# Value columns of two heads as one Strassen product, the second head's values parked in DRAM

## The chip, the cores and the metric

One Trainium2 chip, one core of it. The metric is the device time of one execution in microseconds (us). Engines by their names in the profile: PE is TensorE's matmuls and PEld its weight loads, DVE is VectorE, ACT is ScalarE, POOL is GpSimd, SP issues the transfers. Lines (L1269) are those of the kernel's file.

## What is computed

One layer of a hybrid decoder: a norm, one input projection for everything, three kinds of head groups side by side, a gate, an output projection with a residual, a last norm. Sizes: 1024 tokens, model width 1024, input projection 1024 x 6160, all in float32.

```python
h = rms_norm(x, norm_w)
proj = h @ w_in                              # (1024, 6160)
gq, gk, gv, glr, hq, hf, hi, xq, gate = split(proj)
gla_o  = rms_norm(chunked_gla(gq, gk, gv, log_decay(glr)))       # 4 heads, keys 128, values 256
hgrn_o = rms_norm(chunked_gla(hq, 1 - f(hf), hi, log f(hf)))     # 4 heads of 128
xo     = rms_norm(softmax(xq @ mk.T) @ mv)                       # 4 heads of 128, 256 memory rows
mixed  = concat(gla_o, hgrn_o, xo) * silu(gate)                  # (1024, 2048)
return rms_norm(x + mixed @ w_out, final_norm_w)
```

The change concerns `gv` (1024 columns, 256 for each of four GLA heads) and `hi` (512 columns, 256 for each pair of HGRN heads): the columns of `proj` that hold values.

## The kernel before

The work goes in eight groups, each of 256 columns of the mixed row: X0, X1 (memory attention, two heads each), G0 to G3 (one GLA head each), H0, H1 (two HGRN heads each). A group first projects what it needs (values, gates, queries, keys), with the list `first[i]` of small units run by `emit`; then its `loop` goes over eight chunks of 128 tokens, and between the chunks it does the output projection of the group before (`out_units`, 96 matmuls in 16 units, each into one of three "pp" banks; the sums go through DRAM: fetched into "acc", added at L1997, written back).

Products are exact to float32 by parts: each operand is kept as a high and a low part, and `mm3` (L1498) issues three matmuls, hi x hi, hi x lo, lo x hi (L1500 to L1502). The normed input is kept in such parts as eight sums of its quarters, `self.A`: A11, A12, A22 and S1 to S4, where the first index is the half of the tokens and the second the half of the 1024 channels. These allow Strassen's form of a 2 x 2 product with seven products (`pair`, L1504, used for gate, queries and keys, where the two column blocks of weights are 128 wide). The token quarters are the matmul's moving side there, 512 wide, and the results lie transposed.

The values come from `v_units` (L1597), one group of 256 columns at a time. There the tokens are the stationary side and the weights move, 256 wide. Half of the tokens is A11, A12; for the other half it uses S1 and A22 with the weights changed (c - a, d - b). A group has six operands a, b, c, d, c - a, d - b: the first two serve all eight token blocks (48 matmuls), the other four serve four (24 matmuls). The results fill the four banks "o", "kv", "sc", "tr" and are copied by ACT (L1627) into the tile "v" (one buffer).

Weights pass through one planner, `Fast.load`, `add`, `prepare`, `w` and `w_done` (L1233 to L1288). A load brings 128 x 512 floats (256 KB) on SP's queue into one of five raw buffers "wst" (`NRAW`). An operand is made from one raw, or from a sum of raws that is done in place (L1262, DVE), and then a cast (L1269, ACT) and a low part (L1270, DVE) into one of five slots "whi"/"wlo" (`NSLOT`). `w(i)` asks for operand i and has two more made ahead (`LOOKAHEAD`). Raw buffers go round, and so do slots: load n takes the buffer of load n - 5 when its last reader is done, operand n the slot of operand n - 5 when its last matmul is done. The order of instructions on each engine is a list made when the kernel is built: units in the order of the source have precedence, but what is not ready yet is overtaken.

Other names in the steps: the tail is what is left of the group before (`step_C`: norm, and two gate units with transposes into the bank "oT", L982, L987); it is run in the first units of the next group's `emit`. The background `bg` holds the pieces that turn gates into decays (`decays`, L1740: scans, two `inverse` of Ln and Exp, L1735 to L1738, and in H groups `keys`, L1862): six pieces in a G group, sixteen in an H group. `emit` (L2064) runs one piece after a unit, in H groups from the 14th unit on after every second one. `gates_gla` (L1697) are the two gate matmuls (L1714) into "pp", read by ACT at L1718 and L1719. "sg" holds four tiles of 128 x 512 (silu of the gates), "h" two, "acc" three.

Of the kernel before, what the change touches and what calls it, by code (L numbers as in the profile page):

```python
# [18 lines left out]
P = 128  # L19
# [1199 lines left out]
class Fast(Trunk):  # L1219
# [35 lines left out]
    def prepare(self, i):  # L1255
# [4 lines left out]
        if sub:  # L1260
            d, a, b = (self.raws[j] for j in sub)
            nc.vector.tensor_tensor(d, a, b, op=ALU.subtract)  # L1262
# [334 lines left out]
    def v_units(self, g, col):  # L1597


        nc, add = self.nc, self.add  # L1600
        a, b = (self.load(("v", col, 256, 0, 4), j) for j in range(2))
        c, d = (self.load(("v", col, 256, 4, 4), j) for j in range(2))
        base = add(a)
        add(b)
        add(c)
        add(d)
        add(c, None, (c, c, a), (a, c))
        add(d, None, (d, d, b), (b, d))
# [455 lines left out]
    def emit(self, g, units):  # L2064
# [3 lines left out]
        for n, u in enumerate(units):  # L2068
# [4 lines left out]
            elif self.bg and (not H or n >= 14 and n % 2 == 0):  # L2073
                self.bg.pop(0)()
# [168 lines left out]
```

## Time and profile before

| | us |
|---|---|
| median of three runs (lowest, highest) | 894.61 (893.73, 897.25) |
| the profiled execution, its own time | 894.56 |
| its span, first to last instruction | 892.8 |
| PE busy | 856.5 (96%) |
| DVE busy | 626.2 (70%) |
| ACT busy | 529.6 (59%) |
| POOL busy | 92.5 (10%) |

Busy times of PE overlap, since matmuls are pipelined and the end of one is modelled; how far apart their starts lie says more. The page cuts the span into 40 slices of 22.3 us. Groups start at about 208 (G0), 306.7 (G1), 406.7 (G2), 505.7 (G3), 605 (H0) and 730 us (H1), each with its values first (in H0 and H1 after the forget gates), then gate and queries, then the loop.

### The profile page before, as it was taken

The numbers are of one execution on the slowest core, as the hardware profiler recorded it, in microseconds if no ns is written. First come the engines' busy times: TensorE is split into PE (matmuls) and PEld (weight loads), VectorE is DVE, ScalarE is ACT, GpSimd is POOL, SyncE is SP. The second block draws the span as 40 slices with busy tenths as digits, with TensorE's granted clock in tenths as the row PEclk, the third lists the DMA queues.
The fourth block names the chain that finished last, engine by engine and source line by source line (L and its number), as shares of the span: only waits on it lengthen the run. The fifth ranks groups of instructions, "written<-read, shape, count | busy, mean of one in ns | idle before, by whom it ended". The sixth has DMA issues, their size and how long they took to land.

```text
span 892.8 us, 13855 instructions
## 1 busy us (share of the span) xinstructions
PE 856.5 (96%) x4742; PEld 714.4 (80%) x4742; DVE 626.2 (70%) x1504; ACT 529.6 (59%) x1273; POOL 92.5 (10%) x111
## 2 busy tenths in 40 slices
PE   8788999999999999999999999999999999999994
PEld 7466887788888898888888898878977878877873
DVE  5879663657648885788648875787685777666676
ACT  4536967987435764467436754466963358942374
POOL 0212112321000110011000110011000011000012
PEclk9989999999999999999999999999999999999997
DMA  9410222451225612472235511473113561034764
GB/s 321 163 48 0 62 69 63 162 199 41 78 84 189 213 49 66 134 236 87 79 107 189 190 60 59 153 229 103 48 48 122 176 208 38 25 110 135 265 220 183
DMA packets 61120, 111.84 MB, mean 125 GB/s; under 512 B 6960, under 2 KB 7088, under 8 KB 61040
## 3 DMA queue, kind: packets, MB, share of 16 engines
q1 hardware_dynamic: 60752, 110.59, 37.4%
q8 instruction: 39, 0.64, 0.3%
q14 instruction: 41, 0.34, 0.1%
q10 hardware_dynamic: 288, 0.28, 0.1%
HBM read 77.28 MB, written 33.55 MB: 124 GB/s over the span
## 4 chain that ended last, share of the span: by engine, by line
PE 69%; DVE 13%; DMA 7%; ACT 7%; issue 3%; SPq 0%; POOL 0%; DVEq 0%; POOLq 0%; ACTq 0%
PE pp L1502 16%; PE pp L1500 16%; PE pp L1501 16%; DMA acc<-sum 3%; DVE acc L1997 2%; PE sc L1500 1%; PE o L1500 1%; DVE A L177 1%; PE sc L1502 1%; DMA A<-w_dram 1%; PE sc L1501 1%; DMA A<-xT_dram 1%; PE oT L982 1%; PE o L1501 1%; PE o L1502 1%
## 5 line engine op out<-in xcount | busy, mean ns | idle before, releaser
L1269 ACT CAST whi<-wst 128x512 fp32r<-128x512 f32 x193 | 117.5, 619 | 181.2 <-PE pp L1501 125.5
L1500 PE MATMUL pp<-A,whi 128*128 128x512 f32 x508 | 203.5, 402 | 3.1 <-ACT A L176 1.5
L1501 PE MATMUL pp<-A,whi 128*128 128x512 f32 x508 | 202.0, 398 | 2.2 <-DVE A L177 2.2
L1502 PE MATMUL pp<-A,wlo 128*128 128x512 f32 x508 | 201.9, 398 | 1.5 <-DVE wlo L1270 1.4
L1270 DVE TENSOR_TENSOR wlo<-wst,whi 128x512 fp32r<-128x512 f32 x193 | 131.7, 689 | 80.9 <-ACT whi L1269 76.3
L1500 PEld LDWEIGHTS pp<-A,whi 128*128 128x128 f32 x508 | 95.8, 189 | 27.5 <-ACT A L176 2.7
L1502 PEld LDWEIGHTS pp<-A,wlo 128*128 128x128 f32 x508 | 95.7, 188 | 26.4 <-DVE wlo L1270 3.6
L1501 PEld LDWEIGHTS pp<-A,whi 128*128 128x128 f32 x508 | 96.0, 189 | 25.6 <-DVE A L177 3.5
L1500 PE MATMUL pp<-whi,mh 128*128 128x512 f32 (+1 forms) x258 | 104.7, 406 | 0.3 <-DVE acc L1997 0.3
L1501 PE MATMUL pp<-wlo,mh 128*128 128x512 f32 (+1 forms) x258 | 102.7, 398 | 0.0
L1502 PE MATMUL pp<-whi,ml 128*128 128x512 f32 (+1 forms) x258 | 101.9, 395 | 0.6 <-POOL ml L992 0.6
L1997 DVE TENSOR_TENSOR acc<-acc,pp 128x512 f32<-128x512 f32 x112 | 76.6, 685 | 31.9 <-PE pp L1502 14.5
L992 POOL TENSOR_TENSOR ml<-h,mh 128x512 fp32r<-128x512 f32 x30 | 41.1, 1369 | 334.4 <-ACT mh L990 334.3
L1262 DVE TENSOR_TENSOR wst<-wst 128x512 f32<-128x512 f32 x82 | 56.9, 694 | 1.5
L1502 PEld LDWEIGHTS pp<-whi,ml 128*128 128x128 f32 x258 | 48.7, 189 | 10.4 <-POOL ml L992 1.0
L1501 PEld LDWEIGHTS pp<-wlo,mh 128*128 128x128 f32 x258 | 48.8, 189 | 7.8 <-DVE wlo L1270 0.3
L1500 PEld LDWEIGHTS pp<-whi,mh 128*128 128x128 f32 x258 | 48.7, 189 | 7.9 <-DVE acc L1997 0.5
L177 POOL TENSOR_TENSOR qk<-qk 128x128 fp32r<-128x128 f32 x28 | 13.0, 470 | 292.8 <-ACT qk L176 253.6
L1955 ACT ACTIVATE o<-o,rs_r 128x128 f32<-128x128 f32 (+1 forms) x96 | 34.2, 427 | 8.7 <-DVE rs_r L195 6.9
L1949 ACT ACTIVATE junk<-o 128x128 bf16<-128x128 f32 (+1 forms) x96 | 32.7, 342 | 1.1
L1946 ACT COPY o<-o 128x256 f32<-128x256 f32 x64 | 23.6, 369 | 15.7 <-PE o L1918 4.7
L990 ACT CAST mh<-h 128x512 fp32r<-128x512 f32 x32 | 19.8, 618 | 21.2 <-DVE h L987 21.1
(278 smaller groups left out, 1860.9 us busy)
## 6 DMA issues: line engine op xcount, KB each, us to landing
wst<-w_dram SPq DMA_DIRECT2D x128, 256.0 KB, 2.6
sum<-acc SPq DMA_DIRECT2D x112, 256.0 KB, 2.1
acc<-sum SPq DMA_DIRECT2D x96, 256.0 KB, 2.8
A<-w_dram SPq DMA_DIRECT2D x16, 256.0 KB, 5.4
A<-xT_dram SPq DMA_DIRECT2D x16, 256.0 KB, 5.4
acc<-x_dram SPq DMA_DIRECT2D x16, 256.0 KB, 2.9
A<-sum SPq DMA_DIRECT2D x16, 256.0 KB, 4.0
out_dram<-A SPq DMA_DIRECT2D x15, 256.0 KB, 2.1
```

Source lines behind the costliest of these rows:

```text
L177: eng.tensor_tensor(to[1], x, to[0].bitcast(F32), op=ALU.subtract)
L992: eng.tensor_tensor(lo, x, hi.bitcast(F32), op=ALU.subtract)
L1262: nc.vector.tensor_tensor(d, a, b, op=ALU.subtract)
L1269: nc.scalar.copy(hi, x)
L1270: nc.vector.tensor_tensor(lo, x, hi.bitcast(F32), op=ALU.subtract)
L1500: mm(out, lhs[0], rhs[0], start=first, stop=False, skip_group_check=skip)
L1501: mm(out, lhs[0], rhs[1], start=False, stop=False, skip_group_check=skip)
L1502: mm(out, lhs[1], rhs[0], start=False, stop=last, skip_group_check=skip)
L1946: nc.scalar.copy(osb, o)
L1949: nc.scalar.activation(junk[:, s * w : (s + 1) * w], osb[:, s], AF.Square, accum_out=g["ss"][:, c % 4, s : s + 1])
L1955: self.nc.scalar.activation(x, x, AF.Copy, scale=r)
L1997: nc.vector.tensor_tensor(dst, dst, ps, op=ALU.add)
```

## The change

The values of two groups (G0 with G1, G2 with G3, H0 with H1) are projected together, by `v_pair` in the first group of each pair, with Strassen's seven products; the two 256-column blocks of weights are the two columns of the 2 x 2 form. Each product has two operands (the two 128-channel pairs of a half), and each operand serves four token blocks, 24 matmuls. The 14 operands of a pair are made from 1, 1, 2, 2, 3, 3, 1, 1, 2, 2, 1, 1, 4, 4 raw loads, 28 in all, and 14 sums (the planner now takes a list of sums, also additions). Six banks are used, the four from before and "oT" and one "pp". Partial results lie in four "sg" tiles (u, u4), and the last ones are added from PSUM by DVE (`plus`) or copied by ACT. The first group's values go to "v" directly, the second group's through an "h" tile to DRAM in four writes of 256 KB. The second group has one unit in the place of its values, `v_load`: four reads of 256 KB into "v". In `emit`, the background of H1 (n = 1) runs after every unit from the 14th on instead of every second one.

```diff
--- before.py
+++ after.py
@@ -1257,9 +1257,9 @@
         raw, need, sub, free, make = self.ops[i]
         while self.n_load <= need:
             self.issue(self.n_load)
-        if sub:
-            d, a, b = (self.raws[j] for j in sub)
-            nc.vector.tensor_tensor(d, a, b, op=ALU.subtract)
+        for *sab, op in [(*sub, ALU.subtract)] if type(sub) is tuple else sub or ():
+            d, a, b = (self.raws[j] for j in sab)
+            nc.vector.tensor_tensor(d, a, b, op=op)
         if make:
             self.slots[i] = make(self.raws[raw])
         else:
@@ -1594,42 +1594,114 @@
 
         return [part(n, q) for n in range(8) for q in range(2)]
 
-    def v_units(self, g, col):
-
-
...
         st = {}
 
-        def part(p, j):
+        def put(e, h, ps, u):
+            for i in range(2):
+                src = ps[i].rearrange("p a b -> p (a b)")
+                if e == 0:
+                    dst = g1["v"][:, 4 * h + 2 * i : 4 * h + 2 * i + 2].rearrange("p a b -> p (a b)")
+                else:
+                    dst = self.t("h", [P, HALF], bufs=2)
+                if u is None:
+                    nc.scalar.copy(dst, src)
+                else:
+                    self.plus(dst, src, u[i])
+                if e:
+                    n = f"v{2 * h + i}"
+                    t = g2.setdefault("vd", {})[2 * h + i] = self.dp.tile([P, HALF], F32, tag=n, name=n)
+                    nc.sync.dma_start(t, dst)
+
+        def done(p):
+            ps = st["ps"]
+            flat = lambda t: t.rearrange("p a b -> p (a b)")
+            if p == 0:
+                st["u"] = [self.t("sg", [P, HALF], bufs=self.sg_bufs) for _ in range(2)]
+                for i in range(2):
+                    nc.scalar.copy(st["u"][i], flat(ps[0][i]))
+            elif p == 2:
+                st["u4"] = [self.t("sg", [P, HALF], bufs=self.sg_bufs) for _ in range(2)]
+                for i in range(2):
+                    self.plus(st["u"][i], flat(ps[2][i]), st["u"][i])
+                    self.plus(st["u4"][i], flat(ps[1][i]), st["u"][i])
+            elif p == 3:
+                put(0, 0, ps[0], None)
+            elif p == 4:
+                put(1, 1, ps[2], st["u4"])
+            elif p == 5:
+                put(1, 0, ps[1], st["u"])
+            elif p == 6:
+                put(0, 1, ps[2], st["u"])
+
+        def part(p, j, i):
             def f():
-                if p == 0 and j == 0:
-                    g["v"] = self.t("v", [P, NB, 256], bufs=1)
-                    st["ps"] = [self.ps(t, [P, 2, 256]) for t in ("o", "kv", "sc", "tr")]
-                whi, wlo = self.w(base + p, 2)
-                name = ("A11" if j < 2 else "S1") if p < 2 else "A12" if p < 4 else "A22"
-                for i in range(2):
-                    sl = slice((2 * j + i) % 4 * P, ((2 * j + i) % 4 + 1) * P)
+                if p == j == i == 0:
+                    g1["v"] = self.t("v", [P, NB, 256], bufs=1)
+                    st["ps"] = [[self.ps(t, [P, 2, 256]) for t in ts] for ts in (("o", "kv"), ("sc", "tr"), ("oT", "pp"))]
+                whi, wlo = self.w(ops[p][j], 2)
+                name, bank = prods[p]
+                for b in range(2):
+                    sl = slice((2 * i + b) * P, (2 * i + b + 1) * P)
                     for k in range(2):
-                        hi, lo = self.A[name][2 * (p % 2) + k]
-                        first, last = p == 0 and i == k == 0, (p == 3 or p == 5) and i == k == 1
-                        self.mm3(st["ps"][j][:, i], (hi[:, sl], lo[:, sl]), (whi[:, k], wlo[:, k]), first, last, True)
-                if j == (1 if p in (2, 3) else 3):
-                    self.w_done(base + p)
-                if p == (3 if j < 2 else 5):
-                    nc.scalar.copy(g["v"][:, 2 * j : 2 * j + 2], st["ps"][j])
+                        hi, lo = self.A[name][2 * j + k]
+                        first = p not in cont and j == b == k == 0
+                        last = j == b == k == 1
+                        self.mm3(
+                            st["ps"][bank][i][:, b], (hi[:, sl], lo[:, sl]), (whi[:, k], wlo[:, k]), first, last, True
+                        )
+                if i == 1:
+                    self.w_done(ops[p][j])
+                    if j == 1:
+                        done(p)
 
             return f
 
-        js = lambda p: range(4) if p < 2 else range(2) if p < 4 else range(2, 4)
-        return [part(p, j) for p in range(6) for j in js(p)]
+        return [part(p, j, i) for p in range(7) for j in range(2) for i in range(2)]
+
+    def v_load(self, g):
+        def f():
+            g["v"] = self.t("v", [P, NB, 256], bufs=1)
+            v = g["v"].rearrange("p a b -> p (a b)")
+            for i in range(4):
+                self.nc.sync.dma_start(v[:, i * HALF : (i + 1) * HALF], g["vd"][i])
+
+        return [f]
+
+    def v_of(self, g, other, base):
+        n = g["n"]
+        if n % 2:
+            return self.v_load(g)
+        return self.v_pair(g, other, base + 256 * n, base + 256 * (n + 1))
 
     def glr_units(self):
 
@@ -2070,7 +2142,7 @@
             if self.tail:
                 if n in (0, 3, 5) or n > 5:
                     self.tail.pop(0)()
-            elif self.bg and (not H or n >= 14 and n % 2 == 0):
+            elif self.bg and (not H or n >= 14 and (g["n"] or n % 2 == 0)):
                 self.bg.pop(0)()
 
     def loop(self, g, fill):
@@ -2116,10 +2188,10 @@
                     n, kind = g["n"], g["kind"]
                     if kind == "G":
                         u = self.glr_units() if n == 0 else []
-                        u += self.gates_gla(g, n) + self.v_units(g, GV + 256 * n)
+                        u += self.gates_gla(g, n) + self.v_of(g, groups[(i + 1) % 8], GV)
                         u += self.gate_units(g) + self.qk_units(g, n)
                     else:
-                        u = self.hf_units(g, n) + self.v_units(g, HI + 256 * n)
+                        u = self.hf_units(g, n) + self.v_of(g, groups[(i + 1) % 8], HI)
                         u += self.gate_units(g) + self.hq_units(g, n)
                     first.append(u)
                 fill.append(self.out_units(groups[i - 1], False))
```

## Rows read from the trace of the kernel before

**Rows 1.** The page: busy time by engine (share, count); granted clock and GB/s by slice

```profile
PE 856.5 (96%) x4742; PEld 714.4 (80%) x4742; DVE 626.2 (70%) x1504; ACT 529.6 (59%) x1273; POOL 92.5 (10%) x111
...
PEclk9989999999999999999999999999999999999997
...
GB/s 321 163 48 0 62 69 63 162 199 41 78 84 189 213 49 66 134 236 87 79 107 189 190 60 59 153 229 103 48 48 122 176 208 38 25 110 135 265 220 183
```

**Rows 2.** Busy time by stretch: start:end length, each engine (instructions), clock, DMA share, GB/s

```profile
306.66:331.63 24.97, 24.38 (x202) 23.82 (x201) 21.23 (x63) 17.87 (x35) 2.83 (x3) 1.00 0.19 62
331.47:370.84 39.37, 39.37 (x172) 31.65 (x171) 20.49 (x33) 14.61 (x25) 0.93 (x2) 1.00 0.30 89
...
625.76:648.65 22.89, 22.89 (x194) 22.89 (x193) 13.95 (x51) 22.61 (x31) 0.00 (x0) 1.00 0.14 47
648.49:689.79 41.30, 40.16 (x172) 31.14 (x172) 28.65 (x55) 18.15 (x32) 0.00 (x0) 1.00 0.28 85
...
773.59:814.92 41.33, 40.15 (x172) 31.15 (x172) 28.63 (x53) 18.17 (x32) 0.00 (x0) 1.00 0.29 96
```

**Rows 3.** Instructions by line and form: count | busy us, mean ns | idle before, releaser

```profile
L1270 DVE TENSOR_TENSOR wlo<-wst,whi 128x512 fp32r<-128x512 f32 x193 | 131.7, 689 | 80.9 <-ACT whi L1269 76.3 <-PE oT L982 2.1 <-PE pp L1501 2.0
L1269 ACT CAST whi<-wst 128x512 fp32r<-128x512 f32 x193 | 117.5, 619 | 181.2 <-PE pp L1501 125.5 <-DVE wst L1262 23.8 <-issue 18.3
...
L1262 DVE TENSOR_TENSOR wst<-wst 128x512 f32<-128x512 f32 x82 | 56.9, 694 | 1.5
...
L1779 DVE TENSOR_TENSOR sg<-pp,acc 128x512 f32<-128x512 f32 x24 | 16.6, 691 | 15.3 <-PE pp L1502 15.2
...
L1524 ACT COPY acc<-pp 128x512 f32<-128x512 f32 x17 | 9.9, 585 | 1.5 <-PE pp L1502 1.5
```

**Rows 4.** The page's DMA issues: count, KB each, us from issue to landing

```profile
wst<-w_dram SPq DMA_DIRECT2D x128, 256.0 KB, 2.6
```

**Rows 5.** The waits of SP's queue: us in total, times, longest

```profile
SPq L1244 <- DVE wlo L1270: 236.6, 87, 37.6
```

**Rows 6.** Timeline of PE at the start of G1: start, us, instruction, [idle before]

```profile
306.66 0.28 PE L1500 MATMUL o<-whi,A 128*128 128x256 f32 x1
...
310.25 0.33 PE L982 MATMUL oT<-ident,o 128*128 128x128 f32 x1 [0.59 <-ACT o L1955]
```

**Rows 7.** Timeline of DVE at the start of G1

```profile
308.51 0.69 DVE L1997 TENSOR_TENSOR acc<-acc,pp 128x512 f32<-128x512 f32 x1
...
317.27 0.68 DVE L1270 TENSOR_TENSOR wlo<-wst,whi 128x512 fp32r<-128x512 f32 x1
```

**Rows 8.** Timeline of ACT at the start of G1

```profile
306.32 1.28 ACT L205 ACT_TABLE_LOAD   x1
...
308.20 0.68 ACT L1719 ACTIVATE qk<-pp,nbias 128x512 f32<-128x512 f32 x1
```

**Rows 9.** Timeline of ACT in the values of H0

```profile
628.84 1.28 ACT L1735 ACT_TABLE_LOAD   x1
630.13 0.42 ACT L1735 ACTIVATE qk<-aux 128x256 f32<-128x256 f32 x1
...
645.07 0.60 ACT L1269 CAST whi<-wst 128x512 fp32r<-128x512 f32 x1
...
649.84 0.60 ACT L1269 CAST whi<-wst 128x512 fp32r<-128x512 f32 x1
```

**Rows 10.** Instructions by line on ACT, 625.8 to 648.6

```profile
L1735 ACT ACT_TABLE_LOAD x5 | 6.4, 1283 | 0.1
L1736 ACT ACT_TABLE_LOAD x5 | 6.4, 1283 | 0.1
```

**Rows 11.** Timeline of PE, 33 to 50 us

```profile
40.91 0.70 PE L233 MATMUL sc<-h,ones 128*128 128x256 f32 x2 [3.49 <-DVE h L232]
```

**Rows 12.** Busy time by stretch, as in rows 2, early in the span

```profile
42.00:49.00 7.00, 6.19 (x19) 5.26 (x20) 5.88 (x17) 2.03 (x6) 0.00 (x0) 0.52 0.12 37
```

More of the change, by code (lines that the diff above doesn't have):

```diff
@@ L1595, in pair_direct @@
         return [part(n, q) for n in range(8) for q in range(2)]
-    def v_units(self, g, col):
[L1600 to L1608, printed above, removed]
-        st = {}
-        def part(p, j):
-            def f():
-                if p == 0 and j == 0:
-                    g["v"] = self.t("v", [P, NB, 256], bufs=1)
-                    st["ps"] = [self.ps(t, [P, 2, 256]) for t in ("o", "kv", "sc", "tr")]
-                whi, wlo = self.w(base + p, 2)
-                name = ("A11" if j < 2 else "S1") if p < 2 else "A12" if p < 4 else "A22"
-                for i in range(2):
-                    sl = slice((2 * j + i) % 4 * P, ((2 * j + i) % 4 + 1) * P)
-                    for k in range(2):
-                        hi, lo = self.A[name][2 * (p % 2) + k]
-                        first, last = p == 0 and i == k == 0, (p == 3 or p == 5) and i == k == 1
-                        self.mm3(st["ps"][j][:, i], (hi[:, sl], lo[:, sl]), (whi[:, k], wlo[:, k]), first, last, True)
-                if j == (1 if p in (2, 3) else 3):
-                    self.w_done(base + p)
-                if p == (3 if j < 2 else 5):
-                    nc.scalar.copy(g["v"][:, 2 * j : 2 * j + 2], st["ps"][j])
-            return f
-        js = lambda p: range(4) if p < 2 else range(2) if p < 4 else range(2, 4)
-        return [part(p, j) for p in range(6) for j in js(p)]
@@ new lines, in v_pair, with operand @@
+    def v_pair(self, g1, g2, c1, c2):
+        nc = self.nc
+        B = {"11": c1, "12": c2, "21": c1, "22": c2}
+        minus, plus = ALU.subtract, ALU.add
+        def operand(names, sums):
+            out = []
+            for j in range(2):
+                ids = {n: self.load(("v", B[n], 256, 4 * (n[0] == "2"), 4), j) for n in names}
+                todo = [(ids[d], ids[a], ids[b], op) for d, a, b, op in sums]
+                raws = tuple(ids.values())
+                out.append(self.add(ids[names[0]], raws[-1], todo, raws))
+            return out
+        ops = [
+            operand(["11"], []),
+            operand(["12", "11"], [("12", "12", "11", minus)]),
+            operand(["22", "12", "11"], [("22", "22", "12", minus), ("22", "22", "11", plus)]),
+            operand(["21"], []),
+            operand(["22", "12"], [("22", "22", "12", minus)]),
+            operand(["22"], []),
+            operand(
+                ["21", "22", "12", "11"],
+                [("21", "21", "22", minus), ("12", "12", "11", minus), ("21", "21", "12", plus)],
+            ),
+        ]
+        prods = [("A11", 0), ("S1", 1), ("S2", 2), ("A12", 0), ("S3", 2), ("S4", 1), ("A22", 2)]
+        cont = (3, 5, 6)
+        st = {}
+        def put(e, h, ps, u):
[34 more added lines that the diff above has]
+        def part(p, j, i):
+            def f():
+                if p == j == i == 0:
[5 more added lines that the diff above has]
+                    sl = slice((2 * i + b) * P, (2 * i + b + 1) * P)
+                    for k in range(2):
+                        hi, lo = self.A[name][2 * j + k]
[8 more added lines that the diff above has]
+                        done(p)
+            return f
+        return [part(p, j, i) for p in range(7) for j in range(2) for i in range(2)]
```

## The prediction

> **What bounds the kernel now.** I read the page first. Its busy table gives TensorE 96% of the span against 70% for VectorE and 59% for ScalarE, and the slices show the full clock nearly throughout [rows 1]. A share of busy time over pipelined matmuls proves little, so I then asked for the busy time by stretches, cut where the work of TensorE changes. In the stretch of the first H group's values (625.76 to 648.65) TensorE is busy for all of 22.89 us, and that is exactly 192 matmuls of 256 columns: 22.89 / 192 = 0.119 us each, back to back. The next 168 matmuls of 512 columns (gate and queries of a G group) fill 39.37 us, or 0.234 us each, again without a hole [rows 2]. So in the projections TensorE sets the pace, and a matmul removed there is worth its 0.119 us, as long as its operands come in time. VectorE is not far behind in the stretch that opens a G group: 21.23 us busy of 24.97, and in the values of the H groups ScalarE is the full one, 22.61 of 22.89 [rows 2].
>
> The profiled execution took 894.56 us (span 892.8 and 1.8 around it); the median of the runs is 894.61, so a sum against 894.6 stands for both.
>
> **What is removed.** Six groups have 192 value matmuls each, 384 for two heads. Seven products of 2 x 2 parts with 12 matmuls each make 336. That is 48 fewer per pair, 144 in all, at 0.119: **17.2 us** of TensorE. Per pair the stage becomes 336 x 0.119 = 40.0 us, and an operand now lasts 24 matmuls, 2.86 us; before, the first two of a group lasted 48 matmuls, 5.7 us.
>
> **What is added per pair.** Operands: 14 against 12, so two casts (0.62) and two low parts (0.69). Sums of raw weights: 14 against 4 (op 1: one, op 2: two, op 4: one, op 6: three, each for two row halves), ten more at 0.69. Evacuations: ten adds on VectorE (0.69, the price of an add from PSUM) and four copies on ScalarE instead of eight (0.585, the row of a same-sized copy) [rows 3]. VectorE gains 22 instructions, some 15 us; ScalarE loses about 1. Weight loads: 28 of 256 KB against 8, each 2.6 us from issue to landing [rows 4], with four writes and four reads of the parked values. In the value stage that is 28 x 0.26 MB in 40 us, 184 GB/s; the page's slices move up to 321 [rows 1], so bandwidth stays. The parked values have a whole group's time on the way, and their four reads are issued some 20 us or more ahead of use; I cost them at nothing. The reads wait for the one "v" buffer, whose last reader (the loop of the group before) is over by then. They and the four writes wait on SP's queue, and weight loads are queued behind them. Today that queue already stands 236.6 us in 87 waits for a raw buffer to be freed by a low part [rows 5], so loads run ahead of their need; if that cover were gone, each late load costs up to its 2.6 us.
>
> **Do the operands come in time?** An operand from four raws needs landing 2.6 + three sums 2.07 + cast 0.62 + low part 0.69 = 6.0 us, against 2.86 us of matmuls. There are five raw buffers, so the second such operand can't load before the first is made: a chain. But five operand slots let the making run up to four operands ahead, 11.4 us, and the list that orders each engine takes what is ready. From op 4's first half to the last operand the tightest chain I find by hand (raw buffer after raw buffer) is 19.4 us, and TensorE takes 9 x 2.86 = 25.7 over it. So the stage doesn't starve by itself; it starves where other work holds VectorE or ScalarE. Four places:
>
> *G0 and G2* (values first). Of the 21.23 us of VectorE in the opening of a G group [rows 2], twelve instructions are of operands (8.3 us), so 13 us are not (norm, gates, decays, tail). Into the time until the ninth operand is wanted, 8 x 2.86 = 22.9 us, now come six low parts, six sums and the four adds of the third product, 16 x 0.69 = 11: together 24. Also the fifth and sixth operands chain through one raw buffer (2.6 + 0.69 + 0.62 + 0.69 = 4.6 us against 2.86). I take 1 us each (0 to 3): **2.0**.
>
> *G1 and G3* (no values). Now gate products follow the two gate matmuls at once, and they need "pp" banks. At 306.66 TensorE starts on values, which sit in other banks [rows 6]. The three pp banks are then held by the last output sum, added only at 308.51 to 309.20 [rows 7], and by the two gate matmuls, the first of which ScalarE has read at 308.20 + 0.68 = 308.88, behind a 1.28 us table load [rows 8]. TensorE thus has nothing from 306.66 to 308.88, 2.2 us. Against that, the 0.59 us for which it waits at 310.25 for a transposed tile [rows 6] falls into the gap. Net 1.6 each (0 to 3.5): **3.2**. VectorE then carries 13 + 14 x 0.69 (six low parts, three sums, five adds) = 22.7 us in the 2.2 + 19.7 us up to the end of the gate products; the lead of the operands (three are made before the stage, the next low part runs at 317.27 [rows 7], about when it is wanted, 308.9 + 3 x 2.8 = 317.3) covers most of that; the end of 3.5 us stands for what it may not cover.
>
> *H0.* ScalarE's chain of Ln and Exp with a table load before nearly each (five loads at one line, five at the other) [rows 9, 10] is what it is full with. An operand whose slot came free 11.4 us into the stage (637.2) was cast only at 645.07, the next (slot at 640.05) at 649.84 [rows 9]: in the engine's order they stand behind that chain. In the changed stage the operands whose slots come free at those points are the ninth and tenth of 14, with three casts and two copies (3.0 us) more ahead of them. Ninth: 645.07 + 3.0 + cast and low part 1.3 = 649.4, 23.6 after the start, wanted at 8 x 2.86 = 22.9. Tenth: 649.84 + 3.6 + 1.3 = 654.7, 29.0, wanted at 25.7. Stall 3 us (0 to 5). Given back: the gate and query stage after it takes 41.30 us where G needs 39.37 [rows 2], since late decays push into it; with a longer value stage they are done. Net 3.0 - 1.9 = **1.1**.
>
> *H1.* The gate products now start where the values stood, beside the same chain, and all 16 decay pieces are issued one per unit. The third query operand takes its slot 14.0 us in, so like the cast at 649.84, with one more cast, a copy, one or two Silu (0.63) and their table loads ahead, 3.1 to 6.3 us: 28.5 to 31.7 us after the start, wanted at 9 x 2.8 = 25.2. I take 5 (0 if casts slip ahead, 11 if the whole chain of 21 us comes first), less the 1.9 given back: **3.1**.
>
> Sum: 17.2 - 2.0 - 3.2 - 1.1 - 3.1 = 7.8 us. 894.6 - 7.8 = **886.8 us**.
>
> A page speaks on the table loads: the Trainium skill, "ScalarE: Activation LUTs", section "What ACT_TABLE_LOAD costs", has 1283 ns for the load and some 1380 ns of drain at each switch. The trace bears out the first and not the second: load at 628.84, the function at 630.13, 1.29 us later [rows 9]. By the page's price the Silu switches in H1 would cost some 3 us more and the time would be near 890.
>
> **The rivals.** *The covers hold.* Casts slip between table loads and the stalls of H0, H1, G0 and G2 vanish, while the late decays still lose their 3.8 us: 894.6 - 17.2 + 3.2 - 3.8 = 876.8 at best, some 880 if a few us stay. For it: TensorE has no hole in any value stage today. Against: the 8 us delay of the cast at 645.07. Chance 0.20.
>
> *ScalarE takes over in the H groups.* H1's gate operands stand behind the whole Ln and Exp chain (11 us), H0's lose 5 and nothing is given back: 894.6 - 17.2 + 2.0 + 3.2 + 5 + 11 = 898.6, or 893 with half of H1's. For it: ScalarE at 99% there. Chance 0.15, nearly all within 0.5%.
>
> *The clock falls in the new gap.* Once TensorE stood idle for 3.49 us before 40.91 [rows 11], and a little later it ran at a granted clock of 0.52 for 7 us [rows 12], its lower level (1.2 GHz) for most of that. If the 2.2 us before 308.88 in G1 and G3 do the same, each costs half of 7 us: 886.8 + 7 = 893.8. That idling lowers the clock is what the Trainium skill says too, "TensorE: Matmul & The Clock Gate", section "Part 1: The HAM clock gate". Against: the gap is shorter, and TensorE is full before and after it. Chance 0.05.
>
> *The operand feed becomes the bound: slower.* If the adds that wait for products hold VectorE's queue, so that an operand is only started when the one before it is consumed, the operands with three and four raws (two of each per pair) stall by their own chain less 2.86: 6.0 - 2.86 = 3.1 for four raws, 0.7 less for three. With the losses above kept (9.4), the four-raw ones alone give 894.6 - 17.2 + 9.4 + 6 x 3.1 = 905.6; with the three-raw ones it is 920. It makes the kernel slower than now as soon as these stalls pass 17.2 - 9.4 = 7.8 us, 2.6 per pair. For it: one raw ring of five, 20 more loads per pair. Against: the run-ahead that [rows 5] shows. Chance 0.13.
>
> *It doesn't do what it says*: the planner moves other work, and stages the diff doesn't touch lose the gain. About 893. Chance 0.02.
>
> **How the numbers follow.** My forecast, 886.8 with its own spread of 883 to 891, has 0.45. 0.5% (about what a measurement can tell from no change) is 4.5 us, so faster means under 890.1. Faster: 0.20 and 0.43 of the forecast's 0.45, with a little of ScalarE's, 0.64. Same: the rest of those, the clock and most of ScalarE's, 0.23. Slower: the feed, 0.13. The range 879 to 897 leaves out the best part of the covers (0.07) and the feed (0.13).
>
> **What would show it.** Value matmuls of 256 columns: 1008 instead of 1152, still 0.119 apart. A hole of about 2 us on TensorE at the start of G1 and G3, ended by ScalarE's read of the gate bank or the last output sum. Waits of TensorE on casts or low parts near the ninth and tenth operand of H0 and at the first query products of H1; gate stage of H0 back at 39.4 us. It would be wrong if value stages show waits on low parts in every product (the feed), if the granted clock falls after a gap, or if the three pairs run hole-free.

## The result, and the profile after

The changed kernel took **899.96 us** (median of six runs, 897.27 to 902.35) beside 895.76 of the kernel before in the same sitting: a ratio of 1.0051, 95% interval 1.0032 to 1.0071. The forecast was 886.8, so it missed by 13 us and on the wrong side, outside its range of 879 to 897. The profiled execution was the longest of the six, 902.35 us with a span of 900.6; against the 892.8 of before it is 7.8 us longer.

The page of the kernel after (busy, share and count by engine; the granted clock by slice):

```profile
PE 851.9 (95%) x4598; PEld 704.6 (78%) x4598; DVE 666.6 (74%) x1570; ACT 538.2 (60%) x1277; POOL 92.1 (10%) x111
...
PEclk9889999999999999999999999999999999989998
```

And its groups of instructions by line and form (count | busy us, mean ns | idle before, releaser):

```profile
L1269 ACT CAST whi<-wst 128x512 fp32r<-128x512 f32 x199 | 120.4, 617 | 190.1 <-PE pp L1501 98.6 <-DVE wst L1262 59.2 <-PE pp L1502 16.6
...
L1262 DVE TENSOR_TENSOR wst<-wst 128x512 f32<-128x512 f32 x112 | 82.1, 733 | 15.3 <-DMA wst<-w_dram 14.0
```

The change did what it says: 4742 matmuls became 4598, 144 fewer [rows 1], 30 more sums of raw weights, six more casts [rows 3]. The new waits show in the last columns. ScalarE now stands idle for 59.2 us before casts that wait for a sum of raws, where it was 23.8, and VectorE, idle for 1.5 us in all before the sums until now, waits 14.0 there for weight loads to land [rows 3].

To see where the time went I read off the timeline of TensorE when the last gate or query product of each group ends, and took the differences from end to end. A pair's first group should grow by 144 x 0.119 = 17.1 us and its second shrink by 192 x 0.119 = 22.8; what is missing to that is lost:

| us | G0 | G1 | G2 | G3 | H0 | H1 |
|---|---|---|---|---|---|---|
| before, end to end | 271.6 | 99.2 | 100.0 | 99.0 | 119.9 | 125.1 |
| after | 295.8 | 77.5 | 119.7 | 78.2 | 140.1 | 112.3 |
| lost against 17.1 / -22.8 | 7.1 | 1.1 | 2.6 | 2.1 | 3.0 | 10.0 |
| predicted loss | 1.0 | 1.6 | 1.0 | 1.6 | 1.1 | 3.1 |

The losses sum to 25.9 against 17.1 us gained, 8.8 too many (behind H1's last query product the kernel after is 0.9 us shorter, 77.0 us against 77.9). Two groups make most of it, H1 and, in this execution, G0. The idle times of TensorE over 0.9 us in the stages of projections are these (timeline of PE after: start, us, instruction, [idle before <- what ended it]):

```profile
223.30 0.39 PE L1501 MATMUL oT<-wlo,A 128*128 128x256 f32 x1 [1.94 <-DVE wlo L1270]
332.37 0.50 PE L1500 MATMUL pp<-A,whi 128*128 128x512 f32 x1 [1.48 <-ACT qk L1791]
414.16 0.50 PE L1786 MATMUL pp<-aux,wup 128*128 128x512 f32 x1 [1.58 <-DVE acc L2069]
529.59 0.50 PE L1500 MATMUL pp<-A,whi 128*128 128x512 f32 x1 [1.50 <-ACT qk L1791]
666.12 0.35 PE L1500 MATMUL oT<-whi,A 128*128 128x256 f32 x1 [3.27 <-ACT whi L1269]
785.78 0.48 PE L1500 MATMUL pp<-A,whi 128*128 128x512 f32 x1 [1.71 <-DVE acc L1527]
793.24 0.50 PE L1500 MATMUL pp<-A,whi 128*128 128x512 f32 x1 [1.62 <-ACT whi L1269]
800.83 0.60 PE L1502 MATMUL pp<-A,wlo 128*128 128x512 f32 x1 [2.16 <-DVE wlo L1270]
808.83 0.50 PE L1500 MATMUL pp<-A,whi 128*128 128x512 f32 x1 [0.95 <-ACT whi L1269]
```

And by stretch (start:end, length, each engine's busy us, clock, DMA share, GB/s): first H0's 336 value matmuls, then H1's gates and queries, 168 matmuls that filled 41.33 us before [rows 2], then two parts of them.

```profile
627.07:672.15 45.08, 40.78 (x338) 40.16 (x337) 35.97 (x94) 30.79 (x46) 0.00 (x0) 1.00 0.47 147
...
772.43:823.64 51.21, 44.48 (x173) 33.28 (x173) 35.94 (x90) 40.27 (x58) 0.00 (x0) 0.93 0.24 78
794.25:797.66 3.41, 3.41 (x9) 2.68 (x9) 0.33 (x1) 3.37 (x5) 0.00 (x0) 0.50 0.26 77
801.08:804.49 3.41, 3.41 (x9) 2.63 (x9) 2.97 (x8) 2.73 (x4) 0.00 (x0) 0.50 0.03 7
```

H1's stage lost its time twice. Its holes sum to 6.7 us (the four above and one of 0.28), and behind two of them the clock was granted at 0.50, its lower level, for 3.41 us each, with matmuls 0.43 us apart instead of 0.234, 1.7 us lost each time. In all the stage is 11.8 us longer than its 168 matmuls; the 1.7 beyond holes and clock lie at the restarts. Against the kernel before the loss is 10.0, since this stage was 1.9 us longer than its matmuls there too. What ScalarE did meanwhile (timeline of ACT, H1):

```profile
785.50 1.28 ACT L1807 ACT_TABLE_LOAD   x1
786.80 0.42 ACT L1807 ACTIVATE aux<-qk 128x256 f32<-128x256 f32 x1
787.23 1.28 ACT L1808 ACT_TABLE_LOAD   x1
788.53 0.51 ACT L1808 ACTIVATE aux<-aux,ln 128x256 f32<-128x256 f32 x1
789.06 1.28 ACT L1885 ACT_TABLE_LOAD   x1
790.35 0.60 ACT L1885 ACTIVATE sg<-pp 128x512 f32<-128x512 f32 x1
790.97 1.28 ACT L1807 ACT_TABLE_LOAD   x1
792.26 0.42 ACT L1807 ACTIVATE aux<-qk 128x256 f32<-128x256 f32 x1
792.58 0.60 ACT L1269 CAST whi<-wst 128x512 fp32r<-128x512 f32 x1
```

Ln, Exp and Silu take turns, each behind a table load. In 775 to 808 there are 15 loads, 19.2 us. The cast that TensorE waits for at 793.24 runs at 792.58, with four loads between it and the cast before (784.88).

The first of the holes, before 785.78, is no late cast. It ends with an add of VectorE that frees a bank, and that add stood behind a step of the decays which had waited for an Exp (timeline of DVE, H1):

```profile
784.61 0.42 DVE L1809 SCALAR_TENSOR_TENSOR kT<-aux,qk 128x256 f32<-128x256 f32 x1 [1.93 <-ACT qk L1808]
784.95 0.68 DVE L1527 TENSOR_TENSOR acc<-pp,acc 128x512 f32<-128x512 f32 x1
```

So the loads reach TensorE in two ways: by casts that come late, and by VectorE's queue, where an Exp that comes late holds up what stands behind it.

In H0 the view names a cast at 666.12, but counted through, operand by operand, that cast is the 14th operand's, and the matmul is the first of the 13th. The 13th had its cast at 660.10 and its low part by 662.26, before TensorE came to it at 662.69. What TensorE lacked was the bank "oT", onto which the last product adds and which an add of the fifth product's result (L1851) had to read first. In VectorE's order that add stood behind the three sums of the 14th operand:

```profile
661.58 0.68 DVE L1270 TENSOR_TENSOR wlo<-wst,whi 128x512 fp32r<-128x512 f32 x1
...
664.69 0.69 DVE L1262 TENSOR_TENSOR wst<-wst 128x512 f32<-128x512 f32 x1
665.29 0.69 DVE L1851 TENSOR_TENSOR h<-oT,sg 128x512 f32<-128x512 f32 x1
```

In all five kernels with a hole at this place TensorE starts 0.14 to 0.15 us after this add ends, and in one of them (four operands made ahead, below) the view names the add itself.

### The profile page after: what moved, and what is told of

Read it like the earlier page. It is cut to its first block, busy times and chain, and to the rows that moved or that the text cites. A ratio compares the mean times of both kernels' runs of the same rounds, so it can differ in the third digit from the quotient of the medians.

```text
span 900.6 us, 13812 instructions
## 1 busy us (share of the span) xinstructions
PE 851.9 (95%) x4598; PEld 704.6 (78%) x4598; DVE 666.6 (74%) x1570; ACT 538.2 (60%) x1277; POOL 92.1 (10%) x111
## 4 chain that ended last, share of the span: by engine, by line
PE 69%; DVE 12%; ACT 9%; DMA 7%; issue 2%; SPq 0%; POOL 0%; DVEq 0%; ACTq 0%; POOLq 0%
PE pp L1500 17%; PE pp L1502 17%; PE pp L1501 17%; DMA acc<-sum 2%; DVE wst L1262 2%; DVE acc L2069 1%; PE o L1976 1%; DVE A L177 1%; DMA A<-w_dram 1%; ACT whi L1269 1%; ACT L1807 1%; DMA A<-xT_dram 1%; PE oT L982 1%; ACT L1808 1%; PE o L1500 1%
## 5 line engine op out<-in xcount | busy, mean ns | idle before, releaser
L1269 ACT CAST whi<-wst 128x512 fp32r<-128x512 f32 x199 | 120.4, 617 | 190.1 <-PE pp L1501 98.6
L1500 PE MATMUL pp<-A,whi 128*128 128x512 f32 x508 | 206.3, 408 | 8.9 <-ACT qk L1791 3.0
L1501 PE MATMUL pp<-A,whi 128*128 128x512 f32 x508 | 203.7, 401 | 2.2 <-DVE A L177 2.2
L1270 DVE TENSOR_TENSOR wlo<-wst,whi 128x512 fp32r<-128x512 f32 x199 | 135.2, 687 | 59.6 <-ACT whi L1269 56.9
L1262 DVE TENSOR_TENSOR wst<-wst 128x512 f32<-128x512 f32 x112 | 82.1, 733 | 15.3 <-DMA wst<-w_dram 14.0
L2018 ACT COPY o<-o 128x256 f32<-128x256 f32 x64 | 23.6, 369 | 17.1 <-PE o L1990 4.7
L177 POOL TENSOR_TENSOR wup<-qk,wup 128x128 fp32r<-128x128 f32 x32 | 20.3, 645 | 107.8 <-ACT wup L176 58.5
```

Source lines behind the costliest of these rows:

```text
L177: eng.tensor_tensor(to[1], x, to[0].bitcast(F32), op=ALU.subtract)
L1262: nc.vector.tensor_tensor(d, a, b, op=op)
L1269: nc.scalar.copy(hi, x)
L1270: nc.vector.tensor_tensor(lo, x, hi.bitcast(F32), op=ALU.subtract)
L1500: mm(out, lhs[0], rhs[0], start=first, stop=False, skip_group_check=skip)
L1501: mm(out, lhs[0], rhs[1], start=False, stop=False, skip_group_check=skip)
```

## The experiments

Theory A: table loads in the H groups delay the casts. Theory B: the feed of operands (more sums through five raw buffers) costs every pair the same. Theory C: a hole in G0 pulls the clock down. Ratios are to the kernel before, timed in the same sitting (895.8 to 896.7 us).

**Which pair loses.** The first kernel keeps the old value products in H0 and H1 (and the old rule of `emit`), the second, with "G" in the condition, in the G groups:

```diff
...
+        if g["kind"] == "H":
+            return self.v_units(g, base + 256 * n)
         if n % 2:
             return self.v_load(g)
...
```

> Only G0/G1 and G2/G3 share a product; the H groups keep their own value products and the old background rule. Theory A (the loss sits in the H pair, in ScalarE's chain of Ln, Exp and Silu with a table load before nearly each): in the two traces the G pairs lost 12.2 of a gross 11.4 us, so this comes out like the kernel before, between -2 and +2 us. Theory B (the feed of operands through five raw buffers costs each pair the same): two thirds of the changed kernel's +4.2 us, so +2.8 us, and without the H pair no hole in H at all. Theory C (a hole in G0 drops the clock there and leaves slow matmuls behind): G0's product again shows matmuls 0.133 us apart for some 30 us after a hole; without that the G pairs alone would gain 4 to 5 us.

> Only H0/H1 share a product (with the new background rule); the G groups keep their own value products. Theory A: the H pair lost 13.0 us against a gross of 5.7 in the traces, so +5 to +7.5 us over the kernel before, with H1's gate products again interrupted by waits on casts and low parts. Theory B: a third of +4.2, so +1.4 us. Theory C says nothing of this kernel unless a hole in H1 drops the clock, as twice in the changed kernel (3.4 us at half clock each).

G pairs alone: 892.77 us, 0.9964 (0.9942 to 0.9985), 3.5 faster. The H pair alone: 905.09, 1.0105 (1.0076 to 1.0134), 8.8 slower. B falls: one pair gains and the other loses. A's ranges were missed too (-2 to +2 and +5 to +7.5 us), the first because it took the G pairs' loss from the one trace with the slow G0. In the trace of the H pair alone H0 loses 4.0 us and H1 10.4, as in the changed kernel. In the trace of the G pairs the hole in G0 is there again, 1.95 us at 221.85, but the clock stays up, and 256-column matmuls follow at the usual spacing. So the half clock of G0 is a matter of the execution. How much of the median it explains is not shown: each kernel has one trace, and the mean granted clock of the changed kernel's six runs is 0.982 to 0.986, with 0.985 in the profiled one, so it was no better in the others on the whole.

**Is it the table loads?** Only in H1, Ln, Exp and Silu become copies (these functions are left out; the engine keeps its instructions). `wide` is 2 in H1:

```diff
...
+        if wide == 2:
+            nc.scalar.copy(out, x)
+            nc.scalar.copy(out, out)
+        else:
+            nc.scalar.activation(out, x, AF.Ln, scale=2.0**54 if wide else 1.0)
+            nc.scalar.activation(out, out, AF.Exp, scale=-1.0, bias=self.ln54 if wide else 0.0)
...
+            if g["kind"] == "H" and g["n"]:
+                nc.scalar.copy(t, ps if u is None else t)
+            else:
+                nc.scalar.activation(t, ps if u is None else t, AF.Silu)
...
```

> The changed kernel with the Ln and Exp of the decays and the Silu of the gates in H1 replaced by plain copies of the same size (these functions of H1 are left out, and the range flag of its keys is taken from the decays alone), so that ScalarE has the same instructions there and no table loads. Theory A (table loads delay the casts): H1's stage of gates and queries, which lost 10.0 us against its ideal, loses at most 2 to 3, and the time falls by 7 to 9 us against the changed kernel, to 890 to 893. Theory B (operands are late because of VectorE or the five raw buffers): H1 still loses 7 or more, and the time stays at 898 to 900.

889.49 us, 0.9917 (0.9888 to 0.9946): 10.5 below the changed kernel. H1's gates and queries, the row of 51.21 above, are now without a hole:

```profile
771.30:810.66 39.36, 39.36 (x171) 31.37 (x171) 35.21 (x95) 18.11 (x38) 0.00 (x0) 1.00 0.32 101
```

VectorE is as busy as before, ScalarE's 40.27 us are 18.11; 15 loads of 1.28 us, 19.2 in all, are gone. The loss in H1 is the loads (the kernel with one table, below, shows it with the functions in place). H0 lost 5.5 us in this trace, 2.5 more than in the changed kernel, with a half clock behind its hole.

What the new rule of `emit` costs by itself was not tried: with a piece only after every second unit the query products of H1 would come ahead of the decays that they multiply.

**Two attempts that kept the loads.** One puts a load of the table with both Ln and Exp ahead of each inverse, the other lets H1's decays start earlier:

```diff
...
+        s = self.act_set("natural_log_exp_and_others") if wide else None
+        with self.tc.issue_after(s) if wide else nullcontext():
...
```

```diff
-            elif self.bg and (not H or n >= 14 and (g["n"] or n % 2 == 0)):
+            elif self.bg and (not H or g["n"] or n >= 14 and n % 2 == 0):
```

> The changed kernel, with one explicit load of the table that has both Ln and Exp ahead of each of the H groups' 16 inverses, so that the Exp needs none of its own. Theory A: 1.28 us of ScalarE less per inverse where Ln and Exp alternated; H1's stage of gates and queries, which lost 9.9 us, gets 3 to 6 us back, H0's 1 to 3: 892 to 896 where the changed kernel took 900. Theory B: casts are not what is late, no change (within 1 us).

> The changed kernel, with H1's decay pieces run from the first unit on in which one is ready instead of from the 14th on. Theory A, if what matters is that Ln and Exp meet the Silu of the gates: about half of the pieces move beside the forget products, H1 loses 3 to 6 us less, 894 to 897. If it only matters that 16 inverses with their loads (about 40 us of ScalarE) have no value products to stand beside: the holes move into the forget products, H1's total within 2 us, 898 to 900. Theory B: no change.

The first: 896.75 us, 1.0007 (0.9989 to 1.0025), just above the 892 to 896 expected. H0 got 4.5 us back and H1 lost 2.6 more, because a load is made even where the table is there already, and Silu still throws it out: 19 loads in H1 instead of 18. The second: 910.5 us, 1.0168 (1.0143 to 1.0194), which no theory had expected. Started early, Ln and Exp meet the Sigmoids of the forget gates and each other, 23 loads in H1, (H1 has eight inverses, not the 16 of the expectation, which are those of both H groups), and the third gate product waits for a cast (783.62) with 11 loads between it and the cast before:

```profile
784.27 0.79 PE L1500 MATMUL pp<-A,whi 128*128 128x512 f32 x1 [10.08 <-ACT whi L1269]
```

**One table for the group.** In each H group one load of the table that has both functions, put behind the last Sigmoid, all Ln and Exp behind it, and H1's Silu (on copies of the banks, as its last unit) behind the last Exp. The decay pieces start later for it, from the 16th unit on in H0 and the 17th in H1 instead of the 14th, which no run separates from the loads. `sigs` and `exps` hold the Sigmoids and the Exps, `s` is the group's load:

```diff
-            elif self.bg and (not H or n >= 14 and (g["n"] or n % 2 == 0)):
+            elif self.bg and (not H or n >= (17 if g["n"] else 16) and (g["n"] or n % 2 == 0)):
+                if H and "lset" not in g:
+                    self.exps = []
+                    with ExitStack() as es:
+                        for x in g["sigs"]:
+                            es.enter_context(self.tc.issue_after(x))
+                        g["lset"] = self.act_set("natural_log_exp_and_others")
...
+        with self.tc.issue_after(s) if s else nullcontext():
...
+        def silu():
+            with ExitStack() as es:
+                for x in self.exps:
+                    es.enter_context(self.tc.issue_after(x))
+                for t in g.get("silu", ()):
+                    nc.scalar.activation(t, t, AF.Silu)
```

> The changed kernel with the same functions, but in each H group one load of the table that has both Ln and Exp, put behind the last Sigmoid, and H1's four Silu put behind the last Exp; 25 of the 27 loads at the Ln and Exp lines are gone from the order of ScalarE. With plain copies in H1 the time was 889.5. Theory A: the same relief with the functions in place, in H1 and in H0 (where the explicit table took 4.4 us off): 884 to 889. If it was not the loads but the time of the functions themselves that delays the casts: 896 to 900.

> The kernel before, with the one table per H group alone. Its value products cover the loads today: what it can win is the 1.9 us by which each H group's gate and query stage is longer than its matmuls, 891.5 to 894. If the cover holds fully: 895 to 896, no change. If this wins as much as the same edit in the changed kernel (10 us or more), the tables were no loss of the change.

In the changed kernel: **884.1 us**, 0.9854 (0.9828 to 0.9880). In the kernel before (without the move of the Silu, which has no need there): 892.12, 0.9954 (0.9935 to 0.9972). Three loads are left per H group, 3.8 us, where the kernel before had 14. (The changed kernel has 23 loads at the Ln and Exp lines, not the 27 of the expectation.) With the tables out of the way the change is worth 892.1 - 884.1 = 8.0 us; with them it cost 4.2. Its H0 values and its H1 gates:

```profile
622.40:662.33 39.93, 39.93 (x338) 39.92 (x337) 38.88 (x103) 18.73 (x37) 0.00 (x0) 1.00 0.57 179
...
762.63:801.98 39.35, 39.35 (x171) 31.36 (x171) 35.22 (x98) 22.09 (x42) 0.00 (x0) 1.00 0.33 101
```

Both stages run at the pace of their matmuls, 336 x 0.119 = 40.0 and 168 x 0.234 = 39.3 us, the first with VectorE at 97%: it keeps up, and little more would fit beside it. In the kernel before with the same edit the gate stage also falls from 41.3 to 39.35 us, which the forecast had read as 1.9 us of late decays. And ScalarE's timeline shows how little it takes:

```profile
764.80 1.28 ACT L205 ACT_TABLE_LOAD   x1
766.10 0.59 ACT L1524 COPY acc<-pp 128x512 f32<-128x512 f32 x1
766.58 0.42 ACT L1808 ACTIVATE qk<-aux 128x256 f32<-128x256 f32 x1
766.90 0.41 ACT L1808 ACTIVATE aux<-qk 128x256 f32<-128x256 f32 x1
767.21 0.50 ACT L1809 ACTIVATE qk<-qk,ln 128x256 f32<-128x256 f32 x1
767.61 0.50 ACT L1809 ACTIVATE aux<-aux,ln 128x256 f32<-128x256 f32 x1
768.01 0.60 ACT L1269 CAST whi<-wst 128x512 fp32r<-128x512 f32 x1
```

The Trainium skill says as much, "ScalarE: Activation LUTs", section "Table sets: the hidden batching unit": tables come in sets, and Ln followed by Exp is one load, since one set has both. The traces agree only where the load is placed by hand: left alone, the 16 Ln and 16 Exp of the two H groups of the kernel after had 12 and 11 loads.

**The holes of the G pairs.** Three edits: four operands made ahead in `v_pair` instead of two; the two gate matmuls of G1 and G3 into the banks "kv" and "tr" instead of two "pp" banks (on the G pairs alone); both together (on the G pairs alone).

```diff
-                whi, wlo = self.w(ops[p][j], 2)
+                whi, wlo = self.w(ops[p][j], 2, 4)
...
-                ps = self.ps("pp", [P, HALF])
+                ps = self.ps(("kv", "tr")[h] if n % 2 else "pp", [P, HALF])
```

> The changed kernel, with four operands made ahead instead of two in the shared value products only, so that sums and low parts precede the decays and scans in VectorE's order. Theory B and C: the 1.94 us hole of G0, the half clock behind it and the 0.133 us spacing go, as does the 1.58 us hole of G2: 4 to 7 us less than the changed kernel, 893 to 896. If the raw ring alone sets when an operand is made: no change. Theory A: G holes are no part of it, H1 unchanged, since H1 has no value product.

> Shared products in the G pairs only, and the two gate matmuls of G1 and G3 write into two banks of the group's loop instead of two of the three that the gate products need. Theory of the prediction (the 1.5 us hole at the start of G1 and G3 is the wait for a bank that ScalarE reads late): both holes go, 2 to 3 us less than with the G pairs alone (which stood 3.5 below the kernel before), so 889.5 to 891.5 beside 896.3. Rival: the first gate product then waits for the last output sum or for an operand instead, no gain over 892.8.

> As the run with the other banks in G1 and G3, and four operands made ahead in the shared products. The holes of 1.95 us in G0 and of 1.2 to 1.6 us in G2 before the third product go too, as they did in the changed kernel with four ahead: 2 to 3 us less again, 887 to 889.5. If the holes only move (VectorE is as full as before): within 1 us of the run without the look ahead.

Four ahead in the changed kernel: 897.67 us, 1.0031 (1.0016 to 1.0047), less of a gain than the 893 to 896 expected. G0's hole is gone (its loss is below 0), but H0 has two, 2.14 and 2.30 us, where it had one of 3.27. They are ended by the adds that read the banks of the fifth product (L1851), onto which the last product adds: VectorE comes to them late, behind sums and low parts made earlier and, the second time, behind a step of the decays that waited 2.42 us for an Exp. Other banks: 892.41, 0.9969 (0.9953 to 0.9986), no more than the G pairs alone, so the rival was right. The 1.5 us at the start of G1 are gone as predicted; then comes the next that is late, a transpose and a cast of the gate products (G1 and G3 together lose 3.6 us in the trace, where they lost 3.8):

```profile
330.35 0.33 PE L982 MATMUL oT<-ident,o 128*128 128x128 f32 x1 [0.31 <-ACT o L2066]
347.69 0.50 PE L1500 MATMUL pp<-A,whi 128*128 128x512 f32 x1 [0.97 <-ACT whi L1269]
```

Both: 890.45, 0.9934 (0.9915 to 0.9953), 2 us from the operands, 1 us short of what was expected.

**All of it.** The edits of the G pairs and the one table, once with the H pair shared and once without (there the Silu and the rule of `emit` stay as in the kernel before):

> The run before this one in the list (one table in the H groups), with the other banks for the gate matmuls of G1 and G3 and four operands made ahead in the shared products. Holes left by the earlier traces: about 1 us in each of G1 and G3, some in H0. 880 to 886; four ahead cost H0 two holes of 2.2 us in the earlier run (adds into tiles that were not free), which would leave it at 885 to 889.

> Shared products in the G pairs only, with the banks, four ahead and the one table per H group. 890.45 less the 0 to 4 us that the table alone wins beside separate H values: 886.5 to 890. Set against the kernel that also shares the values of H0 and H1 it tells what that pair is worth once the tables are out of its way: 5.7 us gross, so 2 to 5 us if its holes are gone, 0 or less if the pair itself is the loss.

**879.90 us**, 0.9814 (0.9789 to 0.9839), and 885.49, 0.9873 (0.9848 to 0.9899). The H pair, which cost 8.8 us in the kernel that shared it alone, is now worth 5.6, of 48 x 0.119 = 5.7 that were to be had. The G pairs, with their two edits, are worth 892.1 - 885.5 = 6.6 of 11.4.

**The hole of G2.** Of what was left, the 1.1 to 1.6 us at G2's gate matmul are ended by the last output sum of G1, which the forecast had not on its list. Two edits of the best kernel ask whether its fetch from DRAM is late: from POOL's queue, and one unit earlier.

```diff
-                nc.sync.dma_start(t, self.a["x"][:, b, h * HALF : (h + 1) * HALF] if src is None else src)
+                (nc.sync if last else nc.gpsimd).dma_start(t, self.a["x"][:, b, h * HALF : (h + 1) * HALF] if src is None else src)
```

```diff
-                fetch(n + (6 if last else 2))
+                fetch(n + (6 if last else 3))
```

> The best kernel so far (879.9), with the fetches of the output sums issued from POOL's queue instead of SP's, where they stand behind weight loads that wait for a raw buffer. If that queue is what makes the last sum of G1 and G3 late: the hole of 1.1 us at the gate matmul of G2 goes, and holes of under 1 us in the loops with it, 877 to 879.5. If the last sum is late because of what VectorE does before it: the hole stays, within 1 us of 879.9. If issuing from POOL costs the fetch itself more time: 881 to 884, with sums waiting on their fetch all through the loops.

> The best kernel so far, with each output sum fetched three units ahead of its use instead of two (there are three buffers). If the fetch is issued too late: the hole at G2 goes, 877 to 879.5. If the queue then stands until the third buffer is written out, weight loads get later: 880 to 884.

From POOL: 907.81 us, 1.0130 (1.0100 to 1.0161), far above all that was expected, with holes of 2.5 to 3.1 us in the loops. The hole at G2's gate matmul doesn't come there, but TensorE reaches it late itself (3.07 us at 415.36, shortly before), so this run doesn't decide. Earlier: 882.74, 0.9859 (0.9838 to 0.9881), worse in the last group, and the hole stays:

```profile
404.71 0.50 PE L1786 MATMUL pp<-aux,wup 128*128 128x512 f32 x1 [1.01 <-DVE acc L2084]
```

So here the fetch isn't what is late. On VectorE's timeline of this run the sum (403.97) follows without idle time on the small steps of the group's norm (402.39 to 403.9): it stands behind them in the engine's order. One of these steps (L202, 128 x 4) lasts 1.08 us here and 1.10 in the best kernel, where the changed kernel has 0.16 at the same place; why is open. The order itself was not changed in a run.

## Why the prediction was wrong

*Right.* The gross, 144 matmuls at 0.119; the H pair brought 5.6 of its 5.7 once nothing else was late. The parked values at nothing: in G1 their reads are issued at 327.6 to 330.7 and land within 4.0 us, while the loop that uses them starts at 373.3. The operand feed does not starve by itself: H0's 336 matmuls took 39.93 us with VectorE at 97%, so the rival that makes it the bound is out (its 905.6 adds up to 905.4). The hole of G1 and G3, 2.2 less 0.6: 1.48 and 1.50 us, ended by ScalarE's read of the gate bank; the loss was 1.1 and 2.1 for the 1.6 each.

*Wrong, and most of the miss: the term of H1*, 3.1 us for a loss of 10.0. With the same 1.9 given back in both, the stall was taken at 5 and measured 11.8. The mechanism was named (casts behind the chain of Ln, Exp and Silu) but mis-sized in three ways. I worked it out for one late operand, the third of the queries. There TensorE waited 0.95 and 0.28 us, but it had waited three times before that, for a bank at the fifth gate product, for the last gate operand and for the first of the queries: five waits, 6.7 us. I had the chain hold up casts alone, but an Exp that comes late also holds VectorE, and with it the add that frees the bank. And I gave the lower clock to the gap of G1 alone, where it didn't come; it came in H1, 3.4 us at half clock behind the waits, twice, 3.4 us lost in all. (The loads themselves grew from 14 to 18, three at the Silu and one at an Exp; I had counted one or two.) The end of my own bound, 11 us if the whole chain comes first, was nearly the value; I had chosen near the low end. The rival "ScalarE takes over", 893 to 898.6, had this and was given 0.15.

*H0*, 1.1 for 3.0. The stall was predicted as 3.0 and came as 3.27, but that the sizes agree is luck. It came at the 13th operand, not the ninth, and not for a cast but for the add of the fifth product, which stood behind sums in VectorE's order. The loads have a part in it: they held the cast of the 11th operand until 654.39, so raw buffers came free only at 655.7, and the sums of the last two operands followed one upon the other until 665.38, with the add behind them. The 1.9 us given back did come (gates at 39.34 us); the rest is another 1 us of waits for the adds of the third product, and the restarts.

*G0 and G2*, 1 each. G0's hole is at the fifth operand, as said (its first with three raws), behind scans on VectorE, and 1.94 us long. I had let the making run four operands ahead, since there are five slots, but `w` asks for two ahead; with four the hole is gone. In six other kernels that keep this stage as the change has it, the loss is 0.5 to 3.1. In the profiled execution it is 7.1, since the clock fell behind the hole and the matmuls stayed slow after it (below). G2 lost 2.6, of which 1.58 is the last output sum, in no step of mine.

By the median, then: 17.1 gained and 17.1 + 4.2 = 21.3 lost, where 9.4 had been forecast; H1 alone is 7 of the 12 between.

## What to carry to other kernels

Work that is "hidden" hides other work too: before removing matmuls, list what runs beside them on the other engines and ask where it goes; here the second group's values were the cover of ten table loads, 12.8 us, in H1 as in H0 [rows 10]. An engine that is full with table loads isn't a bound to plan around, since one load placed by hand behind the last use of the old table (and in H1 the Silu moved behind the last Exp) left three of 14 or 18 and turned a loss of 4 us into a gain of 8 over the old kernel with the same edit. When a stall is sized by one late instruction, ask for the others in the same queue as well, those before it too, and for the engines that wait for that queue. And where a view names what ended a wait, count through whether that instruction belongs to the one that waited.

## What the runs showed of the hardware

*The clock after a hole.* Holes of the same length do not all lower it. Behind the 1.94 us in G0 the granted clock was 0.50 for 3.4 us, behind 1.94 us in the same place of the kernel with the copies again, behind 1.95 us there with the G pairs alone it stayed at 1.00; behind 3.27 us in H0 it stayed too, while behind 3.53 us in the same place of the kernel with the copies it was at 0.50, for 3.4 us. With the hole of 10.08 us it was at 0.50 for 13.7 us, from 2.0 us into the hole on. The Trainium skill has the clock fall when TensorE idles, "TensorE: Matmul & The Clock Gate", section "Part 1: The HAM clock gate"; these rows agree that it follows holes and show that a hole of 2 or 3 us may do it or not.

*A slower spacing at full clock.* After that half clock in G0, 256-column matmuls ran 0.133 us apart until the stage ended at 256, though the clock was granted in full. Two stretches of 14 us of such matmuls, after the drop in G0 and in G2, and the same place in the G pairs alone:

```profile
228.00:242.00 14.00, 14.00 (x107) 14.00 (x106) 9.42 (x15) 4.17 (x7) 0.00 (x0) 1.00 0.65 209
420.00:434.00 14.00, 14.00 (x119) 13.91 (x118) 13.97 (x34) 8.41 (x20) 2.94 (x2) 1.00 0.39 114
```

```profile
224.00:238.00 14.00, 14.00 (x121) 14.00 (x120) 11.15 (x20) 4.18 (x7) 0.00 (x0) 1.00 0.63 194
```

107 matmuls against 119 and 121. Over the 28 us that it lasted it cost 213 x 0.015 = 3.2 us. DMA traffic is not the difference (0.65 and 0.63), and in the 512-column matmuls behind it the spacing was the usual 0.234. Nor is the half clock by itself: in the kernel with the copies it came at the same place for the same 3.4 us, and 121 matmuls followed in 228 to 242. No other trace here shows the slow spacing; what causes it stays open.
